# Splitting weight tiles two k tiles per instruction, with the high parts' matmuls of a pair ahead of the low parts'

## The chip, the cores and the metric

The kernel runs on one NeuronCore of a Trainium2 chip. The metric is the time of one execution in microseconds (us) on the device; where several executions were timed, their median stands. Engines are called as in the profile: PE is TensorE's matmul stream, PEld its weight loads, DVE is VectorE, ACT is ScalarE, POOL is GpSimd, SP is SyncE.

## What is computed

The reference is a model of 256 tokens and width 2048, in float32: two layers of a first block (three kinds of attention, then an output projection), and one layer of a second block (a delta-rule recurrence and a sparse attention, mixed by gates), which ends in an expert layer. The experts' scores are products of low-rank keys, 16 experts of 16,384 are picked per head and token, and the picked experts' outputs are summed:

```python
def first_block(x, norm_g, w_in, ...):
    for l in range(DEPTH):
        h = _rms_norm(x, norm_g[l])
        proj = jnp.einsum('bsd,dn->bsn', h, w_in[l])
        ...
        x = x + jnp.einsum('bsm,md->bsd', mixed, w_out[l])
...
def _peer_ffn(h, w_query, sub_keys, expert_u, expert_v):
    q = (h @ w_query).reshape(B, T, PEER_HEADS, 2, PEER_HALF)
    s = jnp.einsum('bthcq,hcnq->bthcn', q, sub_keys).astype(jnp.float32)
    ...
    act = jax.nn.gelu(jnp.einsum('nd,nhkd->nhk', hx, expert_u[e]), approximate=False)
    return jnp.einsum('nhk,nhkd->nd', gt * act, expert_v[e])
```

Nearly all of the arithmetic is products of an activation of 256 tokens with a large float32 weight matrix.

## The kernel before

Each product is made at float32 accuracy out of three matmuls on a shorter type: activation and weight are each the exact sum of a high part and a low part, and high times high, low times high and high times low are summed in PSUM. The activations' parts are `xh` and `xl`, the weights' are `wh` and `wl`.

Weights stream through SBUF in tiles of 128 rows (a k tile) by up to 512 columns. One DMA on SP's queue brings two k tiles (`KG`, 512 KB) into `raw` (4 buffers; `weights`, L306, and `weights_rows`, L318). `split_w` (L296) then makes the parts of one k tile: ACT casts `raw` to `wh` (L300), and DVE subtracts, `wl = raw - wh` (L303); in one stage (`share` = 3) POOL makes every third `wl`. `wh` and `wl` have four buffers of one k tile each.

`proj_a` (L324) keeps the activation in the array and streams the weight's columns: six matmuls for each k tile (two token tiles, lines L334 to L336). `proj_b` (L343) keeps the weight in the array and streams 256 tokens: for each block of 128 columns three matmuls (L359 on high and high, L360 on low activation and high weight, L361 on high activation and low weight), so that 512 columns make twelve for each k tile, 24 for a pair. All three of a block stand together, so that the first matmul of a k tile needs its `wh`, the third its `wl`. The product of 2 x 1024 columns at the end (L1718 to L1720) has the same triple in four PSUM banks.

Side work goes between the projections' steps: a `tick` is called after each pair of k tiles, or after each k tile where `fine` is set (the recurrence, about 1230 to 1565 us), and emits one step of attention, recurrence, routing or gates. The order of instructions on each engine is fixed when the program is built, by a scheduler that goes by priorities and a model of durations; each engine then works its own list in order and waits on semaphores.

The expert layer has four stretches. The queries and the routing (about 1780 to 2165 us) run beside the first 13 of 32 `up` projections (`proj_b` of `hT` with `peer_uT`). The gates (`peer_gates`, about 2165 to 2655 us) run beside the other 19, 0.9 steps per pair. A step does two tokens: on DVE `eq` (L1544) and `o1` (L1546), on POOL two `o2` (L1551), on PE two matmuls (L1552), then ACT copies the result to `g` (L1556, one buffer), DVE adds to it (L1561) or adds it to `S` (L1564), and POOL multiplies `S` by it (L1562, twice in the later part). The product with `peer_v` (about 2680 to 3397 us) follows, with one group of matmuls for each 128 experts and a last group of two; at its end each token tile's `close` adds the four PSUM banks to the residual (L1691), squares, normalises and stores.

Of the kernel before, what the change touches and what calls it, by code (L numbers as in the profile page):

```python
# [8 lines left out]
F32R = mybir.dt.float32r  # L9
# [6 lines left out]
PSUM = bass.MemoryType.PSUM  # L16

P = 128
T = 256
# [5 lines left out]
KG = 2  # L25

# [59 lines left out]
class Lazy:  # L86
    """n items, made by make(k) (some from k on) when they are asked for."""
# [48 lines left out]
class Pipeline:  # L136
    """Generators through two stages (a yielded True asks for the second), one in each."""
# [20 lines left out]
class Env:  # L158
# [61 lines left out]
    def split_T(self, src, gain, pool=None):  # L220
        """src: PSUM or SBUF [P, T] view -> exact high / low float32r parts of src * gain."""
# [11 lines left out]
    def norm_T(self, gT, xT=None):  # L233
        """Transposed (x * gain) as split parts, made as they are asked for (from xT in DRAM if it is given)."""
# [44 lines left out]
    def norm_scales_T(self):  # L279
        """The same from the tiles of the transposed x."""  # L280
# [15 lines left out]
    def split_w(self, raw):  # L296
        nc, n = self.nc, raw.shape[-1]
        wh = self.wp.tile([P, 512], F32R, name="wh", bufs=4)[:, :n]
        wl = self.wp.tile([P, 512], F32R, name="wl", bufs=4)[:, :n]
        nc.scalar.copy(wh, raw)  # L300
        self.nsplit += 1
        engine = nc.gpsimd if self.share and self.nsplit % self.share == 0 else nc.vector
        engine.tensor_sub(wl, raw, wh)  # L303
        return wh, wl

    def weights(self, W, k0, nk, c0, n):  # L306
        """nk k tiles of the columns from c0 on (or of several (start, width) ranges, n in all) as split parts."""
        raw = self.wp.tile([P, KG, 512], F32, name="raw", bufs=4)[:, :nk, :n]
        at = 0
        if len(W.shape) == 4:  # L310
            self.nc.sync.dma_start(raw, W[c0 // 512, k0 // KG].rearrange("p (k n) -> p k n", k=KG))
            return [self.split_w(raw[:, k]) for k in range(nk)]
# [3 lines left out]
        return [self.split_w(raw[:, k]) for k in range(nk)]  # L316

    def weights_rows(self, W, k0, c0):  # L318
        """1024 columns of the 128 rows from k0 as split parts, 512 columns each."""
        raw = self.wp.tile([P, KG, 512], F32, name="raw", bufs=4)  # L320
        self.nc.sync.dma_start(raw, W[k0:k0 + P, c0:c0 + 1024].rearrange("p (k n) -> p k n", k=2))
        return [self.split_w(raw[:, k]) for k in range(2)]

    def proj_a(self, xT, W, c0, n, evac, tick=None, defer=False):  # L324
        """Token-major product of n <= 512 columns; evac(t, psum[P, n])."""
        nc, K = self.nc, len(xT)
        acc = [self.psA.tile([P, 512], F32, name="acc") for _ in range(NT)]
        for k0 in range(0, K, KG):
            nk = min(KG, K - k0)
            for kk, (wh, wl) in enumerate(self.weights(W, k0, nk, c0, n)):  # L330
                h, lo = xT[k0 + kk]
                for t in range(NT):
                    o, s = acc[t][:, :n], slice(t * P, (t + 1) * P)
                    nc.tensor.matmul(o, h[:, s], wh, start=k0 + kk == 0, stop=False)  # L334
                    nc.tensor.matmul(o, lo[:, s], wh, start=False, stop=False)  # L335
                    nc.tensor.matmul(o, h[:, s], wl, start=False, stop=k0 + kk == K - 1)  # L336
                if tick and (self.fine or kk == nk - 1):
                    tick()
# [6 lines left out]
    def proj_b(self, xT, W, c0, n, evac, tick=None, defer=False):  # L345
        """Transposed product, blocks of <= 128 columns on the partitions; evac(i, psum[P, nb, T], nb)."""
# [3 lines left out]
        for k0 in range(0, K, KG):  # L350
            nk = min(KG, K - k0)
            for kk, (wh, wl) in enumerate(self.weights(W, k0, nk, c0, n)):
                h, lo = xT[k0 + kk]
                for b in range(nb):
                    m = min(P, n - b * P)
                    ch, cl = wh[:, b * P:b * P + m], wl[:, b * P:b * P + m]
                    o = acc[b // 2][:m, (b % 2) * T:(b % 2 + 1) * T]
                    first, last = k0 + kk == 0 and b % 2 == 0, k0 + kk == K - 1
                    nc.tensor.matmul(o, ch, h, start=first, stop=False, skip_group_check=True)  # L359
                    nc.tensor.matmul(o, ch, lo, start=False, stop=False, skip_group_check=True)  # L360
                    nc.tensor.matmul(o, cl, h, start=False, stop=last, skip_group_check=True)  # L361
                if tick and (self.fine or kk == nk - 1):
                    tick()
# [9 lines left out]
def first_setup(e):  # L373
    """Layer-independent tiles of the first block: the relative-position bias with its mask."""
# [34 lines left out]
def softmax_parts(e, S, mask, tag, work=None):  # L409
    """Unnormalised exp of S + mask for both query tiles (S: [P, 384] = 128 | 256 keys), and 1 / row sums."""  # L410
# [16 lines left out]
def transpose_probs(e, w, work=None):  # L427
    """[P, 384] probabilities -> key-major [P, 384]: keys 0..127 x 256 queries | keys 128..255 x queries 128..255."""
# [9 lines left out]
def score_pairs(nc, S, pairs):  # L438
    """S[:, 0:128] and S[:, 128:384] += q^T k over the contraction pairs (qT, kT) of [K, T]."""
# [7 lines left out]
def weighted_values(e, w, vals, name):  # L447
    """Output [dv, T] in PSUM from normalised probabilities and token-major values vals(t) of [P, dv]."""
# [13 lines left out]
def first_layer(e, l):  # L462
# [282 lines left out]
    def mix(src, c0, n, key, factor):  # L745
        """factor * src times the gate tanh's sum, in place of src."""
# [32 lines left out]
LAG = 5, 6          # steps that the two trips through DRAM of the small inverses are given  # L779
RATE = 0.85         # recurrence steps per k tile of the projections beside it  # L780
# [36 lines left out]
def mixer_norm_and_stash(e, xs):  # L817
    """The first block's closing norm joined to the second's opening one; x leaves for DRAM."""
# [15 lines left out]
def token_split(e, src, n, pool=None, gain=None):  # L834
    """[P, NT, n * P] token-major -> n transposed split parts (times the gain); src(k) gives the [P, NT, P] view."""
# [162 lines left out]
def gate(e, hT, r2, br, c, work, tick=None):  # L998
    """tanh(gate / 2) of 512 columns of a branch, a tile per token tile."""
# [10 lines left out]
def gated(e, th, src, wname, c, sink, tick=None):  # L1010
    """(1 + tanh(gate / 2)) * (src @ W) of 512 columns to sink(c, t, sbuf tile)."""
# [163 lines left out]
def key_norms(e, g, zk, par_, rw):  # L1175
    """Per head and token 1 / |removal key| of the blocks from g * GB on."""
# [14 lines left out]
def rwkv_group(e, g, z, z0, par_, blk, work, rw, AR):  # L1191
    """Four heads (two blocks of two): chunked delta-rule recurrence, group norm, bonus, gate.

    A block's matrices hold both heads: "diagonal" places (even, odd head on the same half) and "crossed" ones.
    Stacked along the partitions the values lie even | odd, the corrections U odd | even."""
# [57 lines left out]
    def each(n, lhs, rhs, *more):  # L1253
        """One PSUM bank: per block the sum of lhs(b)^T rhs(b) over the given pairs, n columns."""
# [102 lines left out]
    def operands(c):  # L1357
        """The chunk's values (token-major) and, but for the last, its keys and removal keys transposed."""
# [90 lines left out]
RC = 52             # expert rows gone through beside the routing; the gates go beside the rest  # L1449
# [363 lines left out]
```

## Time and profile before

| | us |
|---|---|
| time, median of 3 runs | 3410.3 (3410.05 to 3414.73) |
| span of the profiled execution (first to last instruction) | 3409.5 |
| PE busy in it | 3342.1 (98%) |
| DVE, ACT, POOL busy in it | 2351.0, 1807.5, 668.9 |
| `wl` on DVE (L303), 2135 instructions | 1424.8 |
| `wh` on ACT (L300), 2204 instructions | 1308.3 |

The page gives the profiled execution's span and no other time of its own; the median of the runs is 0.8 us longer than the span. Matmuls overlap in the array, so a matmul's own duration (0.28 us for 256 columns) is longer than the distance from one to the next, and a stall shorter than this overlap does not show as idle time of PE. A row of waits tells which engine waited, at which line, for whom, how long in all, how often, and the longest.

### The profile page before, as it was taken

Reading aid. Unit: us, or ns where it says so; the run is one execution under the profiler, and the core shown is the slowest. Engines: PE = TensorE matmul, PEld = TensorE weight load, DVE = VectorE, ACT = ScalarE, POOL = GpSimd, SP = SyncE. Lnnn points to the kernel's source line nnn. Section 1 sums busy time; section 2 is a strip of 40 time slices with the busy share of each in tenths; the row PEclk is TensorE's granted clock in tenths of the full one; section 3 lists DMA queues with packets and bytes.
Section 4 is the critical chain, followed back from the end, with each engine's and each line's share of the span. In section 5 each row is a group of like instructions: output and inputs, shape, how many; then the busy total and the mean of one; then the engine's idle time right before and its main releaser. Section 6 shows DMA issues by size and latency. Waiting matters only on the chain.

```text
span 3409.5 us, 60242 instructions
## 1 busy us (share of the span) xinstructions
PE 3342.1 (98%) x21528; PEld 3001.9 (88%) x21528; DVE 2351.0 (69%) x5235; ACT 1807.5 (53%) x3728; POOL 668.9 (20%) x747
## 2 busy tenths in 40 slices
PE   9999999999999999999999999999999999999998
PEld 8999889999899978778789999999998888888886
DVE  6657656667665578776667777599999765666665
ACT  5556555555555544444455555565454555555555
POOL 0000000000000021121110333489999100000000
PEclk9999999999999999999999999999999999999999
DMA  7555566554664554445775555555444655555554
GB/s 229 170 172 155 163 176 179 176 158 148 194 182 137 168 156 124 124 131 149 241 243 180 175 168 178 180 167 162 154 161 144 212 193 190 193 191 188 189 188 159
DMA packets 260293, 592.18 MB, mean 174 GB/s; under 512 B 26444, under 2 KB 71840, under 8 KB 259352
## 3 DMA queue, kind: packets, MB, share of 16 engines
q1 hardware_dynamic: 253064, 565.20, 53.3%
q0 software_dynamic: 6928, 23.14, 2.1%
q8 instruction: 168, 2.75, 0.3%
q14 instruction: 133, 1.09, 0.1%
HBM read 574.86 MB, written 13.40 MB: 173 GB/s over the span
## 4 chain that ended last, share of the span: by engine, by line
PE 23%; issue 23%; POOL 5%; DVE 4%; DMA 0%; ACT 0%; POOLq 0%; DVEq 0%; ACTq 0%
PE acc L361 5%; PE acc L360 5%; PE acc L359 5%; POOL o L1551 3%; POOL S L1562 2%; PE acc L334 2%; PE acc L336 2%; PE acc L335 2%; DVE wl L303 1%; PE ps L1259 1%; PE ps L1552 1%; PE ps L1339 0%; DVE cand L1511 0%; DVE g L1561 0%; PE ps L842 0%
## 5 line engine op out<-in xcount | busy, mean ns | idle before, releaser
L303 DVE TENSOR_TENSOR wl<-raw,wh 128x512 fp32r<-128x512 f32 (+4 forms) x2135 | 1424.8, 673 | 860.0 <-ACT wh L300 845.8
L300 ACT CAST wh<-raw 128x512 fp32r<-128x512 f32 (+3 forms) x2204 | 1308.3, 600 | 1227.0 <-PE acc L360 488.0
L361 PE MATMUL acc<-xh,wl 128*128 128x256 f32 (+1 forms) x4168 | 1185.2, 284 | 31.5 <-DVE wl L303 29.6
L359 PE MATMUL acc<-xh,wh 128*128 128x256 f32 (+1 forms) x4168 | 1189.1, 285 | 0.7 <-ACT wh L300 0.7
L360 PE MATMUL acc<-xl,wh 128*128 128x256 f32 (+1 forms) x4168 | 1175.0, 282 | 0.0
L361 PEld LDWEIGHTS acc<-xh,wl 128*128 128x128 f32 (+1 forms) x4168 | 786.5, 189 | 46.6 <-DVE wl L303 42.8
L359 PEld LDWEIGHTS acc<-xh,wh 128*128 128x128 f32 (+1 forms) x4168 | 787.4, 189 | 16.3 <-issue 6.8
L360 PEld LDWEIGHTS acc<-xl,wh 128*128 128x128 f32 (+1 forms) x4168 | 787.2, 189 | 0.6
L334 PE MATMUL acc<-wh,xh 128*128 128x512 f32 (+4 forms) x1128 | 444.0, 395 | 6.6 <-ACT xh L229 6.4
L336 PE MATMUL acc<-wl,xh 128*128 128x512 f32 (+4 forms) x1128 | 431.7, 383 | 1.8 <-DVE wl L303 1.7
L335 PE MATMUL acc<-wh,xl 128*128 128x512 f32 (+4 forms) x1128 | 432.0, 383 | 0.0
L206 POOL TENSOR_TENSOR rs<-rs,half 128x2 f32<-128x2 f32 (+2 forms) x24 | 25.9, 1078 | 1563.1 <-DVE rs L205 1563.1
L1551 POOL TENSOR_SCALAR o<-iota,i2T 128x128 fp32r<-128x128 f32 x256 | 258.9, 1021 | 30.6 <-PE ps L1552 30.3
L334 PEld LDWEIGHTS acc<-wh,xh 128*128 128x128 f32 x1128 | 212.6, 189 | 48.3 <-ACT xh L229 7.9
L336 PEld LDWEIGHTS acc<-wl,xh 128*128 128x128 f32 x1128 | 212.4, 188 | 44.5 <-DVE wl L303 3.4
L335 PEld LDWEIGHTS acc<-wh,xl 128*128 128x128 f32 x1128 | 212.8, 189 | 36.9 <-DVE xl L230 0.9
L1718 PE MATMUL acc<-wh,mh 128*128 128x512 f32 x512 | 202.0, 395 | 0.0
L1719 PE MATMUL acc<-wh,ml 128*128 128x512 f32 x512 | 202.0, 395 | 0.0
L1720 PE MATMUL acc<-wl,mh 128*128 128x512 f32 x512 | 202.0, 395 | 0.0
L1719 PE MATMUL ps<-wh,ml 128*128 128x512 f32 x512 | 202.0, 395 | 0.0
L1718 PE MATMUL ps<-wh,mh 128*128 128x512 f32 x512 | 202.0, 395 | 0.0
L1720 PE MATMUL ps<-wl,mh 128*128 128x512 f32 x512 | 202.0, 395 | 0.0
(463 smaller groups left out, 3654.7 us busy)
## 6 DMA issues: line engine op xcount, KB each, us to landing
raw<-in_w_in_dram SPq DMA_DIRECT2D x280, 512.0 KB, 3.8
raw<-in_peer_uT_dram SPq DMA_DIRECT2D x256, 512.0 KB, 3.5
raw<-in_peer_v_dram SPq DMA_DIRECT2D x256, 512.0 KB, 4.4
raw<-in_w_out_dram SPq DMA_DIRECT2D x96, 512.0 KB, 4.6
raw<-in_w_in_dram SPq DMA_DIRECT2D x72, 256.0 KB, 2.8
raw<-in_w_peer_query_dram SPq DMA_DIRECT2D x32, 512.0 KB, 3.8
raw<-in_w_branch_dsa_dram SPq DMA_DIRECT2D x16, 512.0 KB, 4.5
raw<-in_w_branch_rwkv_dram SPq DMA_DIRECT2D x16, 512.0 KB, 5.4
```

The source lines that it names most:

```text
L300: nc.scalar.copy(wh, raw)
L303: engine.tensor_sub(wl, raw, wh)
L334: nc.tensor.matmul(o, h[:, s], wh, start=k0 + kk == 0, stop=False)
L335: nc.tensor.matmul(o, lo[:, s], wh, start=False, stop=False)
L336: nc.tensor.matmul(o, h[:, s], wl, start=False, stop=k0 + kk == K - 1)
L359: nc.tensor.matmul(o, ch, h, start=first, stop=False, skip_group_check=True)
L360: nc.tensor.matmul(o, ch, lo, start=False, stop=False, skip_group_check=True)
L361: nc.tensor.matmul(o, cl, h, start=False, stop=last, skip_group_check=True)
L1551: nc.gpsimd.tensor_scalar(o2, iota, i2T[:, t0 + k:t0 + k + 1], None, op0=OP.is_equal)
L1718: nc.tensor.matmul(o, h[:, ts], vh, start=j == 0, stop=False)
L1719: nc.tensor.matmul(o, lo[:, ts], vh, start=False, stop=False)
L1720: nc.tensor.matmul(o, h[:, ts], vl, start=False, stop=j == ne - 1)
```

## The change

`split_w` takes the whole `raw` pair. One ACT instruction makes the high parts of both k tiles and one DVE instruction both low parts (two k tiles of up to 512 columns each). `wh` and `wl` become pair tiles with two buffers each (`WB`), the same memory as before. Where `share` is set, two of three pairs give the low part of their second k tile to POOL and the first to DVE, which is again one tile of three.

In `proj_a`, `proj_b` and the last product, the matmuls of a pair are issued in another order: first all that use the high parts (both k tiles), then all that use the low parts. Where `fine` is set the tick that stood between the two k tiles stands between the high and the low matmuls. The number of matmuls and of DMAs, their shapes and the arithmetic are the same. In the last product all four banks' high matmuls come ahead of the four banks' low ones. The three products of `Wkv` (L717) get pair tiles, but keep their order of matmuls. Docstrings are left out too.

```diff
+WB = 2
     def split_w(self, raw):
-        nc, n = self.nc, raw.shape[-1]
-        wh = self.wp.tile([P, 512], F32R, name="wh", bufs=4)[:, :n]
-        wl = self.wp.tile([P, 512], F32R, name="wl", bufs=4)[:, :n]
+        nc, nk, n = self.nc, raw.shape[1], raw.shape[2]
+        wh = self.wp.tile([P, KG, 512], F32R, name="wh", bufs=WB)[:, :nk, :n]
+        wl = self.wp.tile([P, KG, 512], F32R, name="wl", bufs=WB)[:, :nk, :n]
         nc.scalar.copy(wh, raw)
         self.nsplit += 1
-        engine = nc.gpsimd if self.share and self.nsplit % self.share == 0 else nc.vector
-        engine.tensor_sub(wl, raw, wh)
-        return wh, wl
+        if self.share and self.nsplit % self.share and nk == 2:
+            nc.gpsimd.tensor_sub(wl[:, 1], raw[:, 1], wh[:, 1])
+            nc.vector.tensor_sub(wl[:, 0], raw[:, 0], wh[:, 0])
+        else:
+            nc.vector.tensor_sub(wl, raw, wh)
+        return [(wh[:, k], wl[:, k]) for k in range(nk)]
...
     def proj_b(self, xT, W, c0, n, evac, tick=None, defer=False):
...
-            for kk, (wh, wl) in enumerate(self.weights(W, k0, nk, c0, n)):
+            w2 = self.weights(W, k0, nk, c0, n)
+            blocks = [(b, min(P, n - b * P)) for b in range(nb)]
+            out = lambda b, m: acc[b // 2][:m, (b % 2) * T:(b % 2 + 1) * T]
+            for kk, (wh, _) in enumerate(w2):
                 h, lo = xT[k0 + kk]
-                for b in range(nb):
-                    m = min(P, n - b * P)
-                    ch, cl = wh[:, b * P:b * P + m], wl[:, b * P:b * P + m]
-                    o = acc[b // 2][:m, (b % 2) * T:(b % 2 + 1) * T]
-                    first, last = k0 + kk == 0 and b % 2 == 0, k0 + kk == K - 1
-                    nc.tensor.matmul(o, ch, h, start=first, stop=False, skip_group_check=True)
+                for b, m in blocks:
+                    o, ch = out(b, m), wh[:, b * P:b * P + m]
+                    nc.tensor.matmul(o, ch, h, start=k0 + kk == 0 and b % 2 == 0, stop=False, skip_group_check=True)
                     nc.tensor.matmul(o, ch, lo, start=False, stop=False, skip_group_check=True)
-                    nc.tensor.matmul(o, cl, h, start=False, stop=last, skip_group_check=True)
-                if tick and (self.fine or kk == nk - 1):
-                    tick()
+            if tick and self.fine and nk == 2:
+                tick()
+            for kk, (_, wl) in enumerate(w2):
+                h = xT[k0 + kk][0]
+                for b, m in blocks:
+                    nc.tensor.matmul(out(b, m), wl[:, b * P:b * P + m], h, start=False, stop=k0 + kk == K - 1,
+                                     skip_group_check=True)
+            if tick:
+                tick()
...
                     for j, h, lo, v in group:
-                        vh, vl = v[k]
-                        nc.tensor.matmul(o, h[:, ts], vh, start=j == 0, stop=False)
-                        nc.tensor.matmul(o, lo[:, ts], vh, start=False, stop=False)
-                        nc.tensor.matmul(o, h[:, ts], vl, start=False, stop=j == ne - 1)
+                        nc.tensor.matmul(o, h[:, ts], v[k][0], start=j == 0, stop=False)
+                        nc.tensor.matmul(o, lo[:, ts], v[k][0], start=False, stop=False)
+            for t in range(NT):
+                ts = slice(t * P, (t + 1) * P)
+                for k in range(2):
+                    for j, h, lo, v in group:
+                        nc.tensor.matmul(acc[t][k], h[:, ts], v[k][1], start=False, stop=j == ne - 1)
```

`proj_a` is changed in the same way as `proj_b`.

## Rows read from the trace of the kernel before

**Rows 1.** The page's first part: busy us, share of the span, instructions.

```profile
PE 3342.1 (98%) x21528; PEld 3001.9 (88%) x21528; DVE 2351.0 (69%) x5235; ACT 1807.5 (53%) x3728; POOL 668.9 (20%) x747
```

**Rows 2.** Stretches: length, busy us (instructions) by engine, granted clock, DMA.

```profile
core 0: us, PE busy (x) PEld busy (x) DVE busy (x) ACT busy (x) POOL busy (x), PEclk, DMA share, GB/s
0.00:1240.00 1240.00, 1228.91 (x8352) 1122.11 (x8353) 781.79 (x1848) 681.68 (x1558) 29.88 (x50) 1.00 0.59 174
1240.00:1310.00 70.00, 59.30 (x413) 53.75 (x413) 63.87 (x147) 25.50 (x50) 19.87 (x31) 0.93 0.37 109
...
1840.00:2165.00 325.00, 320.35 (x2662) 318.72 (x2662) 229.12 (x723) 171.36 (x281) 94.24 (x70) 0.99 0.54 176
2165.00:2300.00 135.00, 135.00 (x1137) 135.00 (x1136) 115.36 (x250) 79.10 (x140) 99.55 (x106) 1.00 0.53 172
2300.00:2655.00 355.00, 333.60 (x2685) 322.91 (x2684) 328.62 (x701) 178.14 (x354) 348.30 (x374) 1.00 0.48 155
```

**Rows 3.** Waits from 2300 to 2655 us: us in all, times, longest.

```profile
ACT g L1556 <- POOL S L1562: 126.2, 74, 3.1
...
PE acc L361 <- DVE wl L303: 21.3, 32, 1.4
```

**Rows 4.** Groups of instructions, 2300 to 2655 us: busy us, mean ns, idle before.

```profile
L1551 POOL TENSOR_SCALAR o<-iota,i2T 128x128 fp32r<-128x128 f32 x186 | 189.6, 1029 | 3.8 <-PE ps L1552 3.8
L1562 POOL TENSOR_TENSOR S<-g,S 128x128 f32<-128x128 f32 (+14 forms) x188 | 163.0, 887 | 2.9 <-DVE g L1561 2.6
...
L303 DVE TENSOR_TENSOR wl<-raw,wh 128x512 fp32r<-128x512 f32 x210 | 159.0, 763 | 0.7 <-ACT wh L300 0.7
```

**Rows 5.** Groups of instructions, 2655 us to the end, POOL nearly idle.

```profile
L303 DVE TENSOR_TENSOR wl<-raw,wh 128x512 fp32r<-128x512 f32 x530 | 368.3, 695 | 279.8 <-ACT wh L300 274.5 <-PE acc L1719 2.8 <-PE ps L1719 1.4
L1708 DVE TENSOR_TENSOR ml<-S,mh 128x256 fp32r<-128x256 f32 x256 | 107.1, 419 | 0.9 <-PE acc L360 0.2
...
L300 ACT CAST wh<-raw 128x512 fp32r<-128x512 f32 x528 | 328.0, 621 | 320.5 <-PE acc L1719 147.5 <-PE ps L1719 144.8 <-PE acc L360 8.9
L1707 ACT CAST mh<-S 128x256 fp32r<-128x256 f32 x256 | 102.7, 402 | 0.0
```

**Rows 6.** Timeline of one gate step: start us, duration, [idle before <- releaser].

```profile
2428.56 0.48 DVE L1561 TENSOR_TENSOR g<-ps,g 128x128 f32<-128x128 f32 x2 [0.90 <-ACT g L1556]
2429.04 0.67 DVE L303 TENSOR_TENSOR wl<-raw,wh 128x512 fp32r<-128x512 f32 x1
2430.39 0.82 DVE L303 TENSOR_TENSOR wl<-raw,wh 128x512 fp32r<-128x512 f32 x1
2431.14 0.68 DVE L1546 TENSOR_TENSOR o<-eq,c 128x512 fp32r<-128x512 f32 x1
2432.21 0.69 DVE L303 TENSOR_TENSOR wl<-raw,wh 128x512 fp32r<-128x512 f32 x1
...
2427.84 1.18 POOL L1551 TENSOR_SCALAR o<-iota,i2T 128x128 fp32r<-128x128 f32 x2
2430.65 2.64 POOL L1551 TENSOR_SCALAR o<-iota,i2T 128x128 fp32r<-128x128 f32 x2
...
2427.89 0.63 ACT L1556 COPY g<-ps 128x256 f32<-128x256 f32 x1 [2.89 <-POOL S L1562]
...
2429.77 0.39 PE L361 MATMUL acc<-xh,wl 128*128 128x256 f32 x1 [0.76 <-DVE wl L303]
2431.06 0.40 PE L1552 MATMUL ps<-o,o 128*128 128x256 f32 x2
```

**Rows 7.** Waits, 1840 to 2165 us, then (last row) 1240 to 1310 us.

```profile
PE acc L361 <- DVE wl L303: 3.0, 3, 2.0
PE acc L361 <- POOL wl L303: 1.4, 1, 1.4
...
PE acc L361 <- DVE wl L303: 5.1, 4, 4.0
```

**Rows 8.** Timeline of DVE in the last group and the end.

```profile
3392.78 0.76 DVE L1691 TENSOR_TENSOR xo<-ps,xo 128x256 f32<-128x256 f32 x2 [0.28 <-PE ps L1720]
...
3394.18 0.76 DVE L1691 TENSOR_TENSOR xo<-ps,xo 128x256 f32<-128x256 f32 x2
...
3398.74 0.75 DVE L1691 TENSOR_TENSOR xo<-ps,xo 128x256 f32<-128x256 f32 x2
```

More of the change, by code (lines that the diff above doesn't have):

```diff
@@ L311, in weights @@
             self.nc.sync.dma_start(raw, W[c0 // 512, k0 // KG].rearrange("p (k n) -> p k n", k=KG))
-            return [self.split_w(raw[:, k]) for k in range(nk)]
+            return self.split_w(raw)
         for c, w in (c0 if isinstance(c0, tuple) else ((c0, n),)):
@@ L315, in weights @@
             at += w
-        return [self.split_w(raw[:, k]) for k in range(nk)]
+        return self.split_w(raw)
     def weights_rows(self, W, k0, c0):
@@ L321, in weights_rows @@
         self.nc.sync.dma_start(raw, W[k0:k0 + P, c0:c0 + 1024].rearrange("p (k n) -> p k n", k=2))
-        return [self.split_w(raw[:, k]) for k in range(2)]
+        return self.split_w(raw)
     def proj_a(self, xT, W, c0, n, evac, tick=None, defer=False):
@@ L335, in proj_a @@
                     nc.tensor.matmul(o, lo[:, s], wh, start=False, stop=False)
+            if tick and self.fine and nk == 2:
[3 more added lines that the diff above has]
+                for t in range(NT):
+                    o, s = acc[t][:, :n], slice(t * P, (t + 1) * P)
                     nc.tensor.matmul(o, h[:, s], wl, start=False, stop=k0 + kk == K - 1)
-                if tick and (self.fine or kk == nk - 1):
-                    tick()
+            if tick:
+                tick()
         def end():
@@ L351, in proj_b @@
             nk = min(KG, K - k0)
-            for kk, (wh, wl) in enumerate(self.weights(W, k0, nk, c0, n)):
+            w2 = self.weights(W, k0, nk, c0, n)
+            blocks = [(b, min(P, n - b * P)) for b in range(nb)]
+            out = lambda b, m: acc[b // 2][:m, (b % 2) * T:(b % 2 + 1) * T]
+            for kk, (wh, _) in enumerate(w2):
                 h, lo = xT[k0 + kk]
-                for b in range(nb):
-                    m = min(P, n - b * P)
-                    ch, cl = wh[:, b * P:b * P + m], wl[:, b * P:b * P + m]
-                    o = acc[b // 2][:m, (b % 2) * T:(b % 2 + 1) * T]
-                    first, last = k0 + kk == 0 and b % 2 == 0, k0 + kk == K - 1
-                    nc.tensor.matmul(o, ch, h, start=first, stop=False, skip_group_check=True)
-                    nc.tensor.matmul(o, ch, lo, start=False, stop=False, skip_group_check=True)
-                    nc.tensor.matmul(o, cl, h, start=False, stop=last, skip_group_check=True)
-                if tick and (self.fine or kk == nk - 1):
-                    tick()
+                for b, m in blocks:
+                    o, ch = out(b, m), wh[:, b * P:b * P + m]
+                    nc.tensor.matmul(o, ch, h, start=k0 + kk == 0 and b % 2 == 0, stop=False, skip_group_check=True)
+                    nc.tensor.matmul(o, ch, lo, start=False, stop=False, skip_group_check=True)
+            if tick and self.fine and nk == 2:
+                tick()
+            for kk, (_, wl) in enumerate(w2):
+                h = xT[k0 + kk][0]
+                for b, m in blocks:
+                    nc.tensor.matmul(out(b, m), wl[:, b * P:b * P + m], h, start=False, stop=k0 + kk == K - 1,
+                                     skip_group_check=True)
+            if tick:
+                tick()
         def end():
@@ L1716, in peer @@
                     for j, h, lo, v in group:
-                        vh, vl = v[k]
-                        nc.tensor.matmul(o, h[:, ts], vh, start=j == 0, stop=False)
-                        nc.tensor.matmul(o, lo[:, ts], vh, start=False, stop=False)
-                        nc.tensor.matmul(o, h[:, ts], vl, start=False, stop=j == ne - 1)
+                        nc.tensor.matmul(o, h[:, ts], v[k][0], start=j == 0, stop=False)
+                        nc.tensor.matmul(o, lo[:, ts], v[k][0], start=False, stop=False)
+            for t in range(NT):
+                ts = slice(t * P, (t + 1) * P)
+                for k in range(2):
+                    for j, h, lo, v in group:
+                        nc.tensor.matmul(acc[t][k], h[:, ts], v[k][1], start=False, stop=j == ne - 1)
             group = []
```

## The prediction

> **What bounds the kernel now.** I read the page's busy times first. PE is busy in 98% of the span [rows 1], so halving the instructions of DVE and ACT can give no more than the time in which PE waits. All 21,528 matmuls stay, with the same shapes. Next come the stretches. From 2165 to 2300 us PE is busy throughout and issues 1137 matmuls in 135 us, 0.119 us each; in the first 1240 us it misses 11.1 us [rows 2]. The time lies in two places: the gates from 2300 to 2655 us, where PE misses 21.4 us, and 1240 to 1310 us, where it misses 10.7; the routing misses 4.7 [rows 2].
>
> Then the waits. In the gates PE waits for `wl` alone, 21.3 us in 32 waits [rows 3]. That makes DVE look like the culprit, but POOL's two kinds of work there take 189.6 and 163.0 us with only 6.7 us of idle time ahead of them in 355 [rows 4], so POOL sets the pace: 93 steps (186 `o2`) at 3.8 us. The step in the timeline shows how. ACT's copy of `g` waits for POOL's product (2.89 us); DVE's add waits 0.90 us for the copy; `wl` stands behind the add in DVE's list and ends at 2429.71, and PE starts at 2429.77 after 0.76 us [rows 6]. It is the low part of a pair's second k tile: from 2429.77 to the step's own matmuls at 2431.06 the three other blocks fit at 0.119 us per matmul, and no further k tile.
>
> POOL is slowed by DVE in turn. Two `o2` take 1.18 us, mostly while DVE stands still, and 2.64 us when DVE runs `wl`, `o1` and `wl` (0.82, 0.68 and 0.69 us, about 2.0 of it beside them) [rows 6]. POOL lost 1.46 us to 2.0 us of DVE, about 0.7 for one. `wl`, for its part, takes 763 ns beside POOL and 695 where POOL is nearly idle [rows 4, 5].
>
> **The change, part by part.**
>
> *Fewer instructions.* A low part takes 695 ns for 512 columns and 419 for 256 [rows 5]: 1.08 ns a column and 143 ns fixed. A pair is then about 1.25 us instead of 1.39. On ACT 621 and 402 ns [rows 5] give 0.86 ns a column, 183 ns fixed, 1.06 us for a pair instead of 1.24. Outside DVE's crowded stretches both savings lie beside PE and count nothing. In the gates 105 pairs (210 tiles [rows 4]) save DVE 105 x 0.143 = 15.0 us, and at 0.7 POOL gets back 10.5 us. I take -10.5. Bounds: nothing, if the fixed part never held POOL up; and -26, if PE stopped waiting at all (21.4 us, and about 0.11 us after each of the 32 waits, 3.5 in all, and 1 for waits too short to show: the matmul at 2429.77 lasts 0.39 us, while two of L1552 in a row take 0.40, so 0.28 each [rows 6]).
>
> The Trainium skill ("VectorE: DVE Perf Modes", the section on the TRN2 errata) gives a float32 tensor_tensor of N columns as (N + 151) / 0.96 ns and says that many small tiles pay the fixed part each. That is 691 ns at 512, beside 695 in the trace, and an estimate of 158 ns saved per pair: 105 x 0.158 x 0.7 = 11.6 us instead of 10.5.
>
> *Another order of matmuls.* In a pair of 24, `wl` of the first k tile was needed by the 3rd matmul and of the second by the 15th; now both by the 17th. The first gains 14 x 0.119 = 1.67 us of time and the second 0.24. The stalls of the gates are the second kind, and there POOL's pace, not the deadline, repeats the wait; the 0.24 us is gained once. In the routing PE waits 3.0 us for DVE and 1.4 for POOL in four visible waits [rows 7]. If each gains 0.24 and the earlier end (0.14), that is 1.5; if half of them are of the first k tile, up to 3. I take -3. The matmul rate itself I leave at 0.119: the triple of three operands and its repeat run at one pace throughout the 135 us.
>
> *High parts come later.* The first matmul of a pair now waits for 1.06 us of ACT instead of 0.62, and its buffer comes free at the 16th matmul instead of the 11th, 0.6 us later: 1.0 us of lead lost. ACT is busy 171.4 of 325 us in the routing [rows 2], so most pairs have it to spare; behind the routing's other work on ACT some may not. Bounds 0 and +5 (one in ten of the 111 pairs that 2662 matmuls make, at 0.44); I take +1.5, near the lower end, because no row shows PE waiting for `wh` there [rows 7].
>
> *The recurrence.* From 1240 to 1310 us DVE is busy 63.9 of 70 us, and PE waits 5.1 us for `wl`, 4.0 of it at once [rows 7], behind a run of other DVE work. Some 14 pairs (413 matmuls with the recurrence's own [rows 2]) save 14 x 0.143 = 2.0 us. Against this the two ticks of a pair are now 16 and 8 matmuls apart instead of 12 and 12: 0.48 us less for every second step of a chain that waits for DVE and ACT. Bounds -5 (the whole wait for `wl`) and +9 (a quarter of the second steps, 75 of the 150 that 176 k tiles at 0.85 make, late by 0.48); I take -1. The granted clock there is 0.93 and in the routing 0.99 [rows 2], so some of it ran at the lower level, 1.2 GHz, behind such waits; I count no change.
>
> *Ends.* In the last group of 24 the four banks were complete at matmuls 6, 12, 18 and 24; DVE took up the first two at 3392.78 and 3394.18, 0.233 us a matmul [rows 8]. Now they are complete at 18, 20, 22 and 24, so the second bank comes 8 x 0.233 = 1.9 us later. The closing chain of the first token tile hangs on it, and DVE took the second token tile's last bank only at 3398.74, after that chain [rows 8]. Bounds 0 (DVE fills its waits with the other banks) and +1.9; I take +1.5. In the other projections the first bank is complete 0.48 us later; that counts only where PE waits for something made of it. I take +1 in all, between 0 and +2.
>
> *Sum.* -10.5 - 3 + 1.5 - 1 + 1.5 + 1 = -10.5 us, which makes the span 3399.0; the median lay 0.8 above the span: about **3400**.
>
> **The rivals.**
>
> *POOL's pace stays.* The same elements cross, and the fixed 143 ns were hidden behind POOL's own start-up. Then the gates give nothing and the rest is zero: 3410. For it: DVE's idle 0.90 us in a step shows that DVE has time; against it: `wl` is lengthened by POOL.
>
> *PE stops waiting.* If two low parts in one piece let POOL and DVE fall into a better rhythm, PE is the bound in the gates too: 3410.3 - 26 = 3384. For it: PE's stretch before ran without a gap at POOL 99.55 of 135 us [rows 2]; against it: POOL has only 6.7 us to give [rows 4].
>
> *The long piece holds up the add (slower).* POOL's next product waits for the copy (0.63) and the adds (0.48), 1.1 us, which its two `o2` cover (1.18 alone) [rows 6]. If the pair's 1.25 us stands between copy and add in DVE's list, the chain is 2.4 us, while the `o2`, slowed by 0.7 x 1.25, take 2.06: POOL idles about 0.35 us. From 30 of the 93 steps on (30 x 0.35 = 10.5) the gain is gone; in 85 of them the kernel takes 3399.8 + 29.8 = 3430, in half 3416. For it: the cast now ends 0.44 us later, so a scheduler places `wl` differently; against it: one `wl` stands behind the add now.
>
> The Trainium skill ("SBUF — State Buffer", Who interferes with whom) says that a DVE instruction with two SBUF inputs and a GpSimd instruction that reads SBUF exclude each other, the second to start waiting for the whole of the first. The 1.18 and 2.64 us agree. By it the pair is one long hold, which is this rival's mechanism; and if all holds are serial, the whole 15.0 us is gained, 3395.3, instead of 10.5.
>
> **How the numbers follow.** Forecast 0.45 (3390 to 3405), POOL's pace 0.26 (3405 to 3413), PE stops waiting 0.13 (3378 to 3390), the add held up 0.16 (3412 to 3430). The range 3382 to 3416 leaves out the lower half of the third and about half of the fourth, nearly 2 in 10. A measurement tells 0.2%, 6.8 us. Faster than 3403.5: nearly all of the forecast (0.41) and the third, 0.54. Within 0.2%: the rest of the forecast and the second, with a little of the fourth, 0.31. Slower: 0.15.
>
> **What would show it.** After: half the instructions of L300 and L303 at about 1.06 and 1.25 us; from 2300 us on a gate step of about 3.7 us instead of 3.8; POOL's `o2` and products shorter on average; PE's waits for the low parts fewer but not gone; the last DVE add about 1.5 us further from PE's end. If the gates shorten by over 20 us, POOL wasn't the pace; if POOL idles at its products for DVE's adds, the slower rival holds; a matmul distance other than 0.119 us, or PE waits for `wh`, would break the sum.

## The result, and the profile after

The changed kernel takes 3443.9 us, the kernel before 3410.2 beside it: ratio 1.0098, 95% interval 1.0083 to 1.0112. It is 1% slower; the forecast was 3400, the range ended at 3416.

The first part of the page of the changed kernel (span 3442.5 us), to be read against [rows 1]:

```profile
PE 3358.4 (98%) x21528; PEld 3005.3 (87%) x21528; DVE 2218.9 (64%) x4202; ACT 1628.4 (47%) x2626; POOL 711.0 (21%) x747
```

DVE has lost 132 us and ACT 179 us of work. POOL has the same 747 instructions and 42 us more in them.

Where the 33 us of span went, from the two traces: each stage ends at the last matmul of its projections. The columns e1 to e8 are the experiments below; differences to before in us, each from one profile.

| stage | before, us | after | e1 order | e2 pairs | e3 subs single | e4 casts single | e8 single from gates |
|---|---|---|---|---|---|---|---|
| first block, both layers | 931.1 | +1.8 | -0.1 | +5.0 | +2.9 | +2.9 | +2.1 |
| to the recurrence | 283.7 | +0.3 | -0.1 | +0.7 | +0.1 | +0.4 | +0.4 |
| recurrence (three projections) | 466.3 | +16.7 | -0.9 | +13.6 | +0.9 | +8.1 | +14.3 |
| output projection, queries | 188.9 | +1.6 | +0.3 | +16.0 | +5.0 | +1.7 | +3.7 |
| routing | 312.5 | -2.9 | -6.9 | +15.4 | -3.7 | -4.3 | -2.9 |
| gates | 500.3 | +12.0 | -14.2 | +9.7 | -14.2 | +11.1 | -14.1 |
| last product | 713.8 | +1.7 | +0.1 | +1.1 | +3.2 | +0.3 | +1.8 |
| end | 13.0 | +1.8 | +2.4 | +0.1 | +1.8 | +1.8 | +1.8 |
| span | 3409.5 | +33.0 | -19.4 | +61.7 | -4.0 | +22.0 | +7.0 |

Profiles of the same code can differ by some 3 us in a stage: e8, which ahead of the gates is the changed kernel, is 2.4 us apart from it in the recurrence and 2.1 in the output projection. The gates and the recurrence carry 28.7 of the 33. The gates first. Stretch 2300 to 2655 us of the changed kernel, columns as in [rows 2], then its waits, as in [rows 3], and its groups, as in [rows 4]:

```profile
2300.00:2655.00 355.00, 330.70 (x2637) 317.73 (x2636) 295.46 (x583) 162.33 (x243) 349.93 (x364) 1.00 0.46 151
```

```profile
ACT g L1574 <- POOL S L1580: 162.3, 78, 3.4
DVE g L1579 <- ACT g L1574: 55.1, 43, 1.6
...
PE ps L1570 <- DVE o L1564: 13.0, 22, 0.8
PE acc L371 <- ACT wh L302: 8.4, 12, 1.4
PE acc L378 <- DVE wl L308: 1.8, 7, 0.3
```

```profile
L1569 POOL TENSOR_SCALAR o<-iota,i2T 128x128 fp32r<-128x128 f32 x183 | 188.4, 1039 | 0.0
L1580 POOL TENSOR_TENSOR S<-g,S 128x128 f32<-128x128 f32 (+13 forms) x181 | 165.8, 936 | 5.1 <-DVE g L1579 4.5
...
L308 DVE TENSOR_TENSOR wl<-raw,wh 128x1024 fp32r<-128x1024 f32 x101 | 133.4, 1325 | 0.2 <-ACT wh L302 0.2
```

PE issues 2637 matmuls in the 355 us where it issued 2685 [rows 2]. Its wait for `wl` has fallen from 21.3 [rows 3] to 1.8 us, as the new order was meant to do; it now waits for `o1` and `wh`. DVE is busy 295 us instead of 329 [rows 2], so the saved work is real, but it has become idle time: DVE's add waits 55.1 us for ACT's copy, and the copy waits for POOL's products. Those take 936 ns instead of 887 [rows 4].

One step shows why. Timelines of POOL, DVE and ACT in the changed kernel (start us, duration, [idle before <- releaser]):

```profile
2416.72 1.94 POOL L1580 TENSOR_TENSOR S<-g,S 128x128 f32<-128x128 f32 x2
2418.64 1.18 POOL L1569 TENSOR_SCALAR o<-iota,i2T 128x128 fp32r<-128x128 f32 x2
```

```profile
2416.31 0.48 DVE L1562 TENSOR_TENSOR eq<-iota,i1T 128x256 f32<-128x256 f32 x1
2416.71 1.21 DVE L308 TENSOR_TENSOR wl<-raw,wh 128x1024 fp32r<-128x1024 f32 x1
2419.36 0.47 DVE L1579 TENSOR_TENSOR g<-ps,g 128x128 f32<-128x128 f32 x2 [1.44 <-ACT g L1574]
```

```profile
2418.69 0.64 ACT L1574 COPY g<-ps 128x256 f32<-128x256 f32 x1 [3.03 <-POOL S L1580]
```

The pair's subtraction starts at 2416.71 and POOL's first product 0.01 us behind it. The first of the two products takes 1.67 us and the second 0.31. DVE is done at 2417.92, the products at 2418.66; only then can ACT copy and, at 2419.36, DVE add: 1.44 us of idle DVE. The scene recurs every second step, 7.32 us apart. Between 2300 and 2640 us the trace has 40 products that start while a pair's subtraction runs; they take 1613 ns on average. The 29 that meet no DVE instruction take 358. It goes the other way too: seven products start 0.02 us ahead of a pair's subtraction; they take 0.61 us, and the subtraction 1.67 instead of 1.21.

The Trainium skill ("SBUF — State Buffer", Who interferes with whom) has a DVE instruction with two SBUF inputs and a GpSimd instruction that reads SBUF exclude each other for the whole instruction. The 1.67 us beside 0.31 agree.

### The profile page after: what moved, and what is told of

The parts are those of the page before. It is cut to its first block, busy times and chain, and to the rows that moved or that the text cites. A ratio compares the mean times of both kernels' runs of the same rounds, so it can differ in the third digit from the quotient of the medians.

```text
span 3442.5 us, 56326 instructions
## 1 busy us (share of the span) xinstructions
PE 3358.4 (98%) x21528; PEld 3005.3 (87%) x21528; DVE 2218.9 (64%) x4202; ACT 1628.4 (47%) x2626; POOL 711.0 (21%) x747
## 5 line engine op out<-in xcount | busy, mean ns | idle before, releaser
L308 DVE TENSOR_TENSOR wl<-raw,wh 128x1024 fp32r<-128x1024 f32 (+4 forms) x1033 | 1218.9, 1182 | 813.8 <-ACT wh L302 760.2
L302 ACT CAST wh<-raw 128x1024 fp32r<-128x1024 f32 (+5 forms) x1102 | 1110.7, 1009 | 1293.4 <-PE acc L372 466.9
L371 PE MATMUL acc<-xh,wh 128*128 128x256 f32 (+1 forms) x4168 | 1033.6, 286 | 8.5 <-ACT wh L302 8.4
L372 PE MATMUL acc<-xl,wh 128*128 128x256 f32 (+1 forms) x4168 | 1019.7, 283 | 0.0
L378 PE MATMUL acc<-xh,wl 128*128 128x256 f32 (+1 forms) x4168 | 591.2, 283 | 14.4 <-DVE wl L308 12.5
L378 PEld LDWEIGHTS acc<-xh,wl 128*128 128x128 f32 (+1 forms) x4168 | 534.1, 189 | 22.0 <-DVE wl L308 18.4
L348 PE MATMUL acc<-wl,xh 128*128 128x512 f32 (+4 forms) x1128 | 298.5, 386 | 4.1 <-DVE wl L308 4.0
L1569 POOL TENSOR_SCALAR o<-iota,i2T 128x128 fp32r<-128x128 f32 x256 | 277.1, 1092 | 15.6 <-PE ps L1570 13.3
L1580 POOL TENSOR_TENSOR S<-g,S 128x128 f32<-128x128 f32 (+3 forms) x228 | 207.7, 928 | 7.5 <-DVE g L1579 6.8
L1574 ACT COPY g<-ps 128x256 f32<-128x256 f32 x128 | 81.9, 640 | 201.6 <-POOL S L1580 188.2
```

The lines of the kernel that those rows point to most:

```text
L308: nc.vector.tensor_sub(wl, raw, wh)
L371: nc.tensor.matmul(o, ch, h, start=k0 + kk == 0 and b % 2 == 0, stop=False, skip_group_check=True)
L378: nc.tensor.matmul(out(b, m), wl[:, b * P:b * P + m], h, start=False, stop=k0 + kk == K - 1, skip_group_check=True)
L1569: nc.gpsimd.tensor_scalar(o2, iota, i2T[:, t0 + k:t0 + k + 1], None, op0=OP.is_equal)
L1580: nc.gpsimd.tensor_mul(S[h][:, :m, ts], g[:, a:b], S[h][:, :m, ts])
```

## Experiments

Two theories. LONG: the length of the merged instruction costs. ORDER: the new order of the matmuls, with its uneven ticks, costs. The first four runs take the change apart; each diff is against the changed kernel.

### e1: the order alone

```diff
+        return [self.split_one(raw[:, k]) for k in range(raw.shape[1])]
+    def split_one(self, raw):
-        wl = self.wp.tile([P, KG, 512], F32R, name="wl", bufs=WB)[:, :nk, :n]
+        wl = self.wp.tile([P, 512], F32R, name="wl", bufs=4)[:, :n]
...
-            nc.vector.tensor_sub(wl, raw, wh)
+        engine.tensor_sub(wl, raw, wh)
```

> The high-first order of the matmuls alone: each k tile is split by its own cast and its own subtraction, as before. Theory LONG (what costs is the pair's instruction itself: 1.2 us on DVE's list, with POOL's product behind it in the gates and the recurrence's chain behind it between 1215 and 1700 us): the gates (end of the routing to the first matmul of the last phase) return to 500 +- 4 us instead of 512, the recurrence's three projections to within 4 us of before instead of +17, the total is 3410 +- 5. Rival ORDER (what costs is where the matmuls and the two ticks of a pair stand): the gates stay at 510 or more, the recurrence at +12 or more, the total 3435 to 3444. Mixed: gates from the one, recurrence from the other, 3422 to 3430. The tail's +1.8 us (last DVE add to PE's last matmul) stays under each, since it belongs to the order.

Measured: 3394.5 us, ratio 0.9962 (0.9948 to 0.9976): faster than both. Recurrence -0.9 us, so the uneven ticks cost nothing; ORDER falls. The gates don't return to 500, they fall to 486.1, which neither theory had.

### e2: the pairs alone

The loops of `proj_a`, `proj_b` and the last product are those of the kernel before; in `proj_b`:

```diff
-            for kk, (wh, _) in enumerate(w2):
+            for kk, (wh, wl) in enumerate(self.weights(W, k0, nk, c0, n)):
...
                     nc.tensor.matmul(o, ch, lo, start=False, stop=False, skip_group_check=True)
+                    nc.tensor.matmul(o, cl, h, start=False, stop=last, skip_group_check=True)
```

> The pair instructions alone: cast and subtraction of two k tiles at once, the matmuls in the order of the kernel before (high, low and high of one k tile, then of the next) and the ticks a k tile apart. LONG: gates 510 to 514, recurrence +12 to +20, tail 0, total 3435 to 3445; with the old order the low part of the first k tile is wanted by the 3rd matmul of the pair instead of the 17th, so it may be worse by some 5 us. ORDER: gates 500 or less, recurrence within 4 us of before, total 3400 to 3410.

Measured: 3475.2 us, ratio 1.0199 (1.0182 to 1.0216). LONG is right in sign, and its 3435 to 3445 are 30 us too low: the output projection and the routing lose 15 us each. In the old order the pair's low part is wanted by its third matmul. PE's waits from 1698 to 2235 us, these two stages:

```profile
PE acc L366 <- DVE wl L306: 9.4, 14, 1.1
PE acc L341 <- DVE wl L308: 8.9, 3, 3.8
PE acc L366 <- DVE wl L308: 6.9, 11, 1.0
```

That is 25.2 us of waiting for `wl`, where the kernel before had 4.4 [rows 7]. Over the whole kernel the new order hides part of what the pairs cost; in the gates it doesn't: the pairs cost 9.7 us there in the old order and 26.2 in the new (-14.2 in e1, +12.0 in the changed kernel).

### e3 and e4: which of the two instructions

```diff
-            nc.vector.tensor_sub(wl, raw, wh)
+            for k in range(nk):
+                nc.vector.tensor_sub(wl[:, k], raw[:, k], wh[:, k])
```

```diff
-        nc.scalar.copy(wh, raw)
+        for k in range(nk):
+            nc.scalar.copy(wh[:, k], raw[:, k])
```

The first is e3, where the cast stays one; the second e4, where the subtraction stays one.

> As the changed kernel, but the subtraction on DVE is made per k tile (two of about 0.7 us into the halves of the pair's tile); the cast on ACT stays one instruction for the pair. LONG with DVE as the place: gates 498 to 503, POOL's step 3.8 us instead of 3.97, recurrence +0 to +6, total 3408 to 3418. LONG with ACT as the place (the cast of 1.06 us stands before the copy of g): gates 508 or more, total 3430 to 3442. ORDER: 3435 to 3444.

> As the changed kernel, but the cast on ACT is made per k tile (two of about 0.62 us into the halves of the pair's tile); the subtraction on DVE stays one instruction of about 1.2 us for the pair. LONG with DVE as the place: gates 510 to 514, recurrence +10 to +20, total 3434 to 3446. LONG with ACT as the place: gates 500 to 503, total 3408 to 3420. ORDER: 3435 to 3444.

Measured: e3 3406.5 us, ratio 0.9999 (0.9990 to 1.0009); e4 3433.5, ratio 1.0081 (1.0064 to 1.0098). It is DVE's subtraction: gates 486.1 with two pieces, lower than the 498 to 503 expected, and 511.4 with one. Outside the gates e3 takes 15 us more than e1 (12 by the medians of the runs): 3.0 in the first block, 4.7 in the output projection, 3.2 in the routing, 3.1 in the last product. e3 has the pair's cast and the pair tiles with two buffers, e1 neither. Which of them costs this isn't shown: e4, with pair tiles and single casts, still has the +2.9 of the first block, and a kernel with both single in pair tiles wasn't run. e4's recurrence, +8.1, is under the +10 to +20 expected.

e3 and the changed kernel differ in nothing but the subtraction, and their gates take 486.1 and 512.3 us. From 2300 to 2655 us of e3:

```profile
DVE g L1580 <- ACT g L1575: 5.3, 33, 0.2
...
L1581 POOL TENSOR_TENSOR S<-g,S 128x128 f32<-128x128 f32 x194 | 153.1, 809 | 6.9 <-DVE g L1580 6.9
```

In e3, though, the second piece stands behind the adds in DVE's list. In e1 and e4 the list has the same order in most steps: `eq`, `wl` in two pieces or one, two adds into `g`, one into `S`, `o1` (59 steps in each between 2300 and 2640 us). So it is no other place in the list. Nor is it the pair tiles, which e4 has and e1 doesn't: e3 has them too, at 486.1. Waits and groups from 2300 to 2655 us, of e4:

```profile
DVE g L1580 <- ACT g L1575: 55.1, 41, 1.7
...
L1570 POOL TENSOR_SCALAR o<-iota,i2T 128x128 fp32r<-128x128 f32 x182 | 186.9, 1037 | 0.0
L1581 POOL TENSOR_TENSOR S<-g,S 128x128 f32<-128x128 f32 (+13 forms) x183 | 167.6, 936 | 5.4 <-DVE g L1580 4.8
L309 DVE TENSOR_TENSOR wl<-raw,wh 128x1024 fp32r<-128x1024 f32 x102 | 134.6, 1324 | 0.2 <-ACT wh L303 0.2
```

and of e1, with its stretch:

```profile
2300.00:2655.00 355.00, 347.90 (x2806) 337.78 (x2804) 341.83 (x713) 185.07 (x371) 333.01 (x368) 1.00 0.49 166
```

```profile
DVE g L1578 <- ACT g L1573: 4.6, 29, 0.2
...
L1568 POOL TENSOR_SCALAR o<-iota,i2T 128x128 fp32r<-128x128 f32 x182 | 204.4, 1133 | 1.6 <-PE ps L1569 1.6
L1579 POOL TENSOR_TENSOR S<-g,S 128x128 f32<-128x128 f32 (+13 forms) x186 | 132.8, 733 | 6.7 <-DVE g L1578 6.7
L307 DVE TENSOR_TENSOR wl<-raw,wh 128x512 fp32r<-128x512 f32 x220 | 178.4, 848 | 0.7 <-ACT wh L304 0.5 <-issue 0.2
```

A pair costs DVE 2 x 848 = 1.70 us in e1 and 1.32 in e4, and e1 is the faster by 25 us in the gates. DVE is busy 46 us more of the 355 than in the changed kernel and almost never waits for the copy. The same place in e1, POOL and then DVE:

```profile
2418.97 1.36 POOL L1579 TENSOR_TENSOR S<-g,S 128x128 f32<-128x128 f32 x2
2420.30 1.62 POOL L1568 TENSOR_SCALAR o<-iota,i2T 128x128 fp32r<-128x128 f32 x2
```

```profile
2418.99 1.89 DVE L307 TENSOR_TENSOR wl<-raw,wh 128x512 fp32r<-128x512 f32 x2
2421.03 0.49 DVE L1578 TENSOR_TENSOR g<-ps,g 128x128 f32<-128x128 f32 x2 [0.16 <-ACT g L1573]
```

The products are done 1.36 us after they start, not 1.94; the waiting is on DVE's side, whose two pieces take 1.89, and DVE idles 0.16 us at its add, not 1.44.

### e8: where the length acts

```diff
-    e.share = 0
+    e.share, e.late = 0, 1     # from the gates on
...
-            nc.vector.tensor_sub(wl, raw, wh)
+            for k in range(nk) if self.late else ():
+                nc.vector.tensor_sub(wl[:, k], raw[:, k], wh[:, k])
+            if not self.late:
+                nc.vector.tensor_sub(wl, raw, wh)
```

> The changed kernel with the subtraction per k tile from the start of the gates on, and in pairs ahead of them. If the pieces' length acts where they run, the gates take what they took in e3_subs_single (486 +- 3) and the stages ahead of them what they took in the changed kernel (recurrence +14 to +18 against before): total 3414 to 3424. If the gates' loss came from what the earlier stages handed on (the number of gate steps left, the state of the queues), the gates stay over 500 and the total over 3430.

Measured: 3414.2 us, ratio 1.0019 (1.0010 to 1.0028). Gates 486.2, recurrence +14.3, as the first case said. The length acts where it runs.

### e6 and e7: is the single g the link?

```diff
-        g = oh.tile([P, n, P], F32, name="g", bufs=1)
+        g = oh.tile([P, n, P], F32, name="g", bufs=2)
...
-            sq = oh.tile([P, T], F32, name="sq", tag="g", bufs=1)
+            sq = oh.tile([P, T], F32, name="sq", tag="g", bufs=2)
...
-        raw = self.wp.tile([P, KG, 512], F32, name="raw", bufs=4)
+        raw = self.wp.tile([P, KG, 512], F32, name="raw", bufs=3)
```

> The changed kernel with two buffers of the gates' tile g (and of the square that shares its tag) instead of one; to make room, three buffers of raw weights instead of four. ACT's copy of a step's g then needn't wait for POOL's products of the step before. CHAIN (the pair's subtraction holds the product, the product holds the copy, the copy holds DVE's add, and DVE stands idle 53 of 340 us): DVE's idle time before the add falls under 15 us and the gates to 480 to 500 us from 512. PACE (POOL simply loses more time to the exclusion in all, whatever waits for it): the gates stay at 507 to 514. Stages before the gates may change by a few us through the third raw buffer; the gates are what counts.

> The same two buffers of g (and three of raw) in e5_order_tail. In e1_order DVE idles only 4.6 of 340 us at its add and PE, DVE and POOL are each busy in 97 to 98% of it, so there is little left: gates 478 to 488 us against 486, total 3386 to 3398. If PACE holds, no change in the gates at all.

Measured: e6 3448.1 us, ratio 1.0123 (1.0107 to 1.0138), gates 501.3. e7 3403.4, ratio 0.9985 (0.9975 to 0.9994), gates 478.6; with three raw buffers the stages ahead of the gates take longer (the first block some 12 us in each against the kernel before), so only the gates are compared. In e7 even they aren't free of the third buffer: ACT waits 17.6 us for weights there (2300 to 2655 us). A wait of e6 from 2300 to 2655 us:

```profile
DVE g L1579 <- ACT g L1574: 27.4, 29, 1.5
```

Neither CHAIN nor PACE: 512.3 falls by 11.0, less than half of the 26.2 between the changed kernel and e3, and DVE's idle time halves. The one buffer passes part of the hold on; the rest is there without it, and POOL is busy in 353.8 of e6's 355 us.

### e10: pieces of a quarter

Against e5 (below), in the gates alone:

```diff
-        engine.tensor_sub(wl, raw, wh)
+        m = n // 2 if self.late else n
+        for c in range(0, n, m):
+            engine.tensor_sub(wl[:, c:c + m], raw[:, c:c + m], wh[:, c:c + m])
```

> e5_order_tail with the subtraction in pieces of 256 columns instead of 512, in the gates alone (four pieces to a pair, 0.42 us each by the rows of 256 columns, 1.68 us a pair in place of 1.39). If shorter pieces went on helping by the holds alone, the gates would fall under 483 us. If DVE's own time now sets the pace (it is busy 97% of the gates there, and 105 pairs x 0.29 us are 30 us more), the gates rise to 495 to 515 us and the total to 3401 to 3421. I expect the second.

Measured: 3399.8 us, ratio 0.9976 (0.9967 to 0.9985), gates 493.2. DVE's group and POOL's, and the stretch, 2300 to 2655 us:

```profile
2300.00:2655.00 355.00, 341.80 (x2746) 331.59 (x2745) 351.14 (x924) 180.72 (x363) 325.86 (x371) 1.00 0.47 159
```

```profile
L1581 POOL TENSOR_TENSOR S<-g,S 128x128 f32<-128x128 f32 (+13 forms) x188 | 151.8, 827 | 19.4 <-DVE g L1580 19.3
...
L309 DVE TENSOR_TENSOR wl<-raw,wh 128x256 fp32r<-128x256 f32 x429 | 178.8, 469 | 0.5 <-ACT wh L304 0.4
```

DVE is busy 351 of 355 us, and now POOL waits for DVE, 19.3 us. That is the second case, just under its 495 to 515. The loss is smaller than the 30 us of added work: a piece takes 469 ns beside POOL, so a pair 1.88 us against 1.70 in e1.

### e5 and e9: what is left to gain

e5 is e1 with the last group of 24 matmuls of each half of the last product in the old order (first diff, against e1); e9 adds two buffers of `g` and of the square that shares its tag, in the room of two buffers of `o2` (second, against e5):

```diff
+                        if j >= ne - 2:
+                            nc.tensor.matmul(o, h[:, ts], v[k][1], start=False, stop=j == ne - 1)
...
-                        nc.tensor.matmul(acc[t][k], h[:, ts], v[k][1], start=False, stop=j == ne - 1)
+                        if j < ne - 2:
+                            nc.tensor.matmul(acc[t][k], h[:, ts], v[k][1], start=False, stop=False)
```

```diff
-            o2 = oh.tile([P, P], F32R, name="o2", bufs=4)
+            o2 = oh.tile([P, P], F32R, name="o2", bufs=2)
...
-        g = oh.tile([P, n, P], F32, name="g", bufs=1)
+        g = oh.tile([P, n, P], F32, name="g", bufs=2)
```

> As e1_order (matmuls high parts first, one cast and one subtraction per k tile), but the last group of 24 matmuls of each half of the last phase in the old order, so that the banks are complete at the 6th, 12th, 18th and 24th matmul again. If the tail's +1.8 to +2.4 us (13.0 before, 14.7 to 15.4 in the kernels with the new order) belongs to that one group, the tail returns to 13.0 +- 0.4 and the total is 2 us under e1_order: 3391 +- 3. If the tail belongs to something earlier, it stays at 15 and the total at 3394.

> e5_order_tail with two buffers of g, room made by two buffers of the gates' one-hot tile o2 instead of four; raw weights keep their four buffers. If the single g was worth 7 us of the gates there (478.6 against 486.0 with three raw buffers) and the third raw buffer was what cost the earlier stages, the gates take 477 to 482 us, the other stages what they took in e5_order_tail, the total is 3385 +- 4. If o2 needs its four buffers (POOL waits for PE's matmuls of the step before), the gates are at 486 or more and the total 3392 or more.

Measured: e5 3392.3 us, ratio 0.9958 (0.9944 to 0.9972), end 13.6 us against 15.4 in e1 and 13.0 before. The whole times of e1 and e5 overlap, so the 2 us are read from the end alone. e9 3392.9, ratio 0.9959 (0.9945 to 0.9972), gates 486.0. POOL waits for `o2`'s buffers, as the second case said (waits of e9, 2300 to 2655 us):

```profile
POOL o L1568 <- PE ps L1569: 12.4, 13, 1.8
```

e5 is the version to keep: the change's order without its pairs, with the old order in the last group.

## Why the prediction was wrong

*What bounds the kernel* held: the gates and the stretch from 1240 us are where the change acted, and POOL's products pace the gates.

*Fewer instructions: the durations held, the conversion failed.* In the last product a pair's subtraction takes 1225 ns and its cast 1049 (forecast 1.25 and 1.06 us):

```profile
L308 DVE TENSOR_TENSOR wl<-raw,wh 128x1024 fp32r<-128x1024 f32 x255 | 312.3, 1225 | 267.5 <-ACT wh L302 265.7 <-ACT mh L1725 1.5
L302 ACT CAST wh<-raw 128x1024 fp32r<-128x1024 f32 x255 | 267.4, 1049 | 362.0 <-PE acc L1736 182.6 <-PE ps L1736 178.9 <-PE acc L372 0.5
```

The failed step is "at 0.7 POOL gets back 10.5 us". I read 1.46 us of POOL's loss beside 2.0 us of DVE [rows 6] as a rate, so that less DVE work must give POOL time. Merging the subtractions alone (e3 to the changed kernel) cost 26.2 us in the gates, where I forecast a gain of 10.5. The same rows held the answer: those 2.0 us were three instructions in a row, and an `o2` that meets one of them waits for its end. What POOL loses goes by how long the piece is that it meets. My bounds, 0 to -26, left out the sign.

*The slower rival* (chance 0.16) had the mechanism half right: a long piece beside the products and a late add. It put the piece between copy and add, and POOL idle for 0.35 us a step. In the trace the piece stands ahead of the copy, POOL idles 5.1 us in all, and it is DVE that idles, 55.1. And its price was set against the 10.5 us of gain, which didn't exist.

*Another order*: "there POOL's pace, not the deadline, repeats the wait; the 0.24 us is gained once" failed, for the gain was larger: e1's gates are 14.2 us shorter than before with the same instructions. With the low parts wanted later, the scheduler put `o1` after the adds and both `wl` ahead of them (before, in 51 steps: `eq`, `wl`, `o1`, adds, `wl`), the products shrank from 887 ns [rows 4] to 733, and DVE's wait at its add fell to 4.6 us, from this wait of the kernel before, 2300 to 2655 us:

```profile
DVE g L1561 <- ACT g L1556: 24.5, 28, 1.1
```

By these rows POOL's pace was itself set by where DVE's pieces lay. e3, with its second `wl` behind the adds, has the same 486.1, so of the two moves only that of `o1` is common to both. Which of the two, deadline or list, gave how much wasn't tried. In the routing the order gave -6.9, where I took -3, and the pairs took 4.0 of it back, where I took 1.5 for the later high parts.

*The recurrence*: -1 forecast, +16.7 measured, outside my -5 to +9. My price was on the uneven ticks, which cost nothing (e1 -0.9, e3 +0.9). The subtraction in one piece costs it: +16.7, +14.3, +13.6 and +8.1 in the four kernels of the table that have it there; e3 differs from the changed kernel in it alone. Stretch 1217 to 1700 us of the changed kernel, then its four stretches at the granted clock of 0.50 (1.2 GHz):

```profile
1217.00:1700.00 483.00, 458.98 (x2623) 385.53 (x2623) 332.82 (x605) 186.63 (x322) 79.64 (x123) 0.97 0.48 143
...
1259.50:1269.70 10.20, 5.79 (x27) 5.79 (x28) 9.30 (x20) 2.37 (x4) 2.40 (x5) 0.50 0.46 124
1300.50:1310.70 10.20, 10.20 (x39) 8.02 (x38) 8.82 (x17) 2.82 (x5) 1.94 (x4) 0.50 0.38 116
1372.10:1378.90 6.80, 6.80 (x20) 4.78 (x19) 3.39 (x6) 1.25 (x2) 2.76 (x4) 0.50 0.47 141
1665.70:1669.10 3.40, 3.40 (x10) 2.62 (x9) 2.24 (x3) 0.37 (x1) 0.88 (x2) 0.50 0.75 208
```

and the same stretch of the kernel before, with its two:

```profile
1215.00:1681.00 466.00, 449.01 (x2622) 378.66 (x2621) 339.07 (x709) 204.44 (x425) 81.28 (x123) 0.99 0.49 149
...
1250.70:1254.10 3.40, 3.40 (x9) 2.15 (x7) 3.40 (x9) 0.51 (x1) 1.27 (x2) 0.50 0.00 0
1257.50:1264.30 6.80, 4.66 (x22) 4.66 (x23) 5.49 (x12) 1.52 (x3) 1.88 (x4) 0.50 0.54 136
```

The number of matmuls is the same. Of the 17 us, 10 are PE's own busy time (459.0 against 449.0) and 7 are waits. The half clock accounts for some 8 of the 10. That is an estimate from the distance of matmuls, here in the first of the four stretches:

```profile
1266.00 0.41 PE L372 MATMUL acc<-xl,wh 128*128 128x256 f32 x1
...
1267.92 0.41 PE L371 MATMUL acc<-xh,wh 128*128 128x256 f32 x1
```

Nine steps from one to the next take 1.92 us, 0.213 each against 0.119 at the full clock [rows 2], so 44% of PE's busy time at the half clock is the clock's; of that time there are 26.2 us, and 8.1 before. So "I count no change" of the clock missed about half of the 17. In e8 and e4 PE waits as long in the three projections as in the changed kernel (24.0 and 23.3 us against 24.0; before 17.0), but they run 23.9 and 13.6 us at 0.50 where it runs 30.6: the waiting is much the same, and the clock makes most of the spread from +8.1 to +16.7.

POOL's busy time doesn't rise here (79.6 against 81.3), so the hold on POOL isn't the road; what the rows show is PE waiting longer for `wl` itself (9.7 us against 6.8 before) and for a chain that stands behind the long piece in DVE's list. PE's wait for the chain's `yb` in these stretches, changed kernel, then before:

```profile
PE ps L1448 <- DVE yb L1444: 4.5, 4, 2.0
...
PE ps L1430 <- DVE yb L1426: 0.7, 1, 0.7
```

Timeline of DVE and PE ahead of the fall at 1372.1, changed kernel:

```profile
1368.92 0.18 DVE L1435 TENSOR_TENSOR gn<-rs,cw 128x16 f32<-128x16 f32 x1 [1.46 <-POOL rs L207]
1369.03 1.23 DVE L308 TENSOR_TENSOR wl<-raw,wh 128x1024 fp32r<-128x1024 f32 x1
1370.17 0.68 DVE L1444 TENSOR_TENSOR yb<-ysb,gn 128x512 f32<-128x512 f32 x1
...
1371.01 0.41 PE L1448 MATMUL ps<-cw,yb 128*128 128x64 f32 x2 [2.03 <-DVE yb L1444]
```

`yb` needs `gn`, and then stands behind 1.23 us of `wl` while PE waits 2.03 us for it. That each of the 14 to 17 us arises so is argued from such rows, not shown; and some 3 us differ from profile to profile with a fall of the clock (the last of the three projections is +0.7 in e1, which has no fall there, and +3.5 in e5, which has one of 3.4 us; their code is the same there).

*Ends.* The tail, +1.5 forecast, is +1.8: right, and undone but for 0.6 us by e5's last group. The other ends, +1 forecast, are part of the 5.4 us in the remaining stages.

*High parts come later* was priced in the routing alone. In the gates PE waits 8.4 us for `wh`, a sign that the prediction named as breaking its sum. The remaining stages, +5.4, are +0.2 in e1, but +11.2 in e3 and +5.3 in e4: neither single subtractions nor single casts bring them back as long as the tiles are pairs. That was a smaller missing term; how much of it is the pair's cast and how much the two buffers, and through which wait it acts, stays open.

Sum by measured terms: gates +12.0, recurrence +16.7, routing -2.9, end +1.8, the rest +5.4: +33.0.

## What to carry to other kernels

Before merging small instructions, ask who waits for them to end: an engine that is excluded while one runs, and the chain instruction behind it in the same list. An engine's saved busy time is worth nothing if the merged piece stands in the loop that sets the pace; time that a neighbour loses beside an engine is no rate, it goes by the length of the instruction that it meets. Take a two-part change apart and time each part: here one half is worth -0.4% and the other +2.0%, and together they read as +1.0%, not as their sum, because each half changes what the other costs (in the gates the pairs cost 9.7 us in the old order and 26.2 in the new).

## What the runs showed of the hardware

Of the three lengths of a DVE piece beside POOL that were tried, the middle one is the best. The gates took 511.4 us with subtractions of 1024 columns (e4), 486.1 with 512 (e1) and 493.2 with 256 (e10), though DVE's time for a pair rose all along: 1.32, 1.70 and 1.88 us. At 1024 POOL's products wait (936 ns) and DVE stands idle; at 256 DVE is busy 99% of the time; at 512 PE, DVE and POOL are all busy 94 to 98%.
